# Last down pair of the second feed-forward by seven block products, and the attention projection's sums moved from GpSimd to VectorE with three low parts by transfers

## The chip, the cores and the metric

The kernel runs on one core of one Trainium2 chip. The metric is device time in microseconds (us) of one execution, lower is better. Before the change the median of three runs is 1553.24 us (1552.8 to 1553.64). TensorE (PE) multiplies matrices, VectorE (DVE), ScalarE (ACT) and GpSimd (POOL) work elementwise, and SyncE (SP), ACT and POOL issue DMA transfers from their instruction queues.

## The reference

One layer of a streaming encoder runs over 576 columns: 512 prompt frames and 64 frames of a running stream. Cut to what matters here:

```python
def swiglu_ffn(x, w_gu, w_down):
    gate, up = jnp.split(x @ w_gu, 2, axis=-1)
    return (jax.nn.silu(gate) * up) @ w_down
...
    y_att = o.reshape(b, t, ATT_WIDTH) @ p['w_att_proj']
    merged = jax.nn.sigmoid(g_ml) * y_ml + jax.nn.sigmoid(g_att) * y_att
...
    h = layer_norm(ALPHA * h + mix, p['ln2_g'], p['ln2_b'])
    h = layer_norm(ALPHA * h + 0.5 * swiglu_ffn(h, p['ffn2_w_gu'], p['ffn2_w_down']), p['ln3_g'], p['ln3_b'])
```

The model width is 1024 (8 tiles of 128), the hidden width of a feed-forward 2816 (22 tiles). The change touches two products: the attention projection `o @ w_att_proj`, and the down projection of the second feed-forward with the layer norm after it, which gives the output `y`.

## The kernel before, in words

Activations lie transposed, features on the 128 partitions and the 576 columns along the free dimension. A product in 32-bit floats is made from three faster matmuls: weights and activations are both split into a high part (a copy rounded to the fast type) and a low part (the rest), and hi·hi, hi·lo and lo·hi are summed in PSUM. A high part is one ACT copy. A low part is one DVE subtraction, or, with `add_lo` (line 196), a second ACT copy with scale -1 and then a transfer issued on POOL that adds the source to it.

**Seven products.** Where a weight block of 2 x 2 quarters multiplies an activation block of 2 x 2 quarters, the kernel forms seven quarter products in place of eight, from sums of weight quarters and sums of activation quarters. `seven` (line 1115) does it for two output tiles of a down projection over the hidden tiles 8 to 15, with column halves of 288 (`A` and `B`); `Units.run` does it for gate and up, for input columns, and, as `Projection`, for the attention projection. `Combos` holds the activation sums: `add` (line 787) makes, for block i, a sum tile u (parts t1 and t3) and a sum tile v (parts t2 and t4), each out of two operations on 288 columns.

**The order of the work.** PE's instructions stand in program order; a small planner (`Order`) keeps a model clock of PE and lets delayed callbacks (`later`, `od.bg`) run as PE's matmuls are emitted. The other engines are ordered by a scheduler with priorities (`hot`, `tc.high_priority`), and each then works through its own queue in that order: what waits at the head holds all that is behind it. Weights come in by `pump` (line 233): SP loads a raw tile `wr` (two buffers), ACT and DVE split it into `wh` and `wl` (four buffers, `NWB`). The planned list is written out in `plan_ffn` (line 382). Tiles of 576 columns called `s` come from a pool of 24 slots (line 99); a new tile must wait until the last reader of the slot's old tile is done.

**The attention projection.** While PE still runs the gates `("in", 64+j)`, the background generator `os_split` (line 1806) splits the attention output `OT` into `oh` and `os`, and makes the sums and their parts, the tiles `tx`, with `halves` (line 1823): in each block i first v (`halves(i, 1)`, tile `o`), then u (`halves(i, 0)`, tile `s`). The u sums of the blocks 1 to 3 are begun on POOL by `begin` (line 780), one block ahead, and every low part is a DVE subtraction. Then lines 1855 to 1858 load two gate tiles `s<-gd` on ACT's queue, and `un.run(tail)` starts PE on the projection: a11·b11, a12·b21, the next unit's a11·b11, then s2·t2 (reads all four v tiles), s1·t1 and s3·t3 (read all four u tiles).

**The end of the second feed-forward.** The output tiles 0 to 5 are done by `plain` and `seven`. The last two, 6 and 7, are done by plain `gemm`s in the order (6, columns 0:320), (7, 0:320), (6, 320:576), (7, 320:576), each over 22 hidden tiles, three matmuls each; the six weight chunks are loaded and split twice, once for each column range. `collect` (line 559) adds a finished product to the residual tile and to the sums of the norm. After the first column range, `stats` (line 648) runs while PE is in the second: small matmuls `aux<-onec`, a chain ACT `m`, DVE `var`, POOL `rs`, ACT `dg` and `c`, then `centre` (line 713) on DVE and POOL, a matmul `aux<-dg` (`spread`), and eight `apply` steps (DVE `s<-s,cols,aux`, ACT, and a transfer `out_y` each). The second column range ends with `turned` (line 682): sums, transposes, eight DVE steps and four transfers `out_yt`; nothing comes after it.

## Time and profile before

| | |
|---|---|
| profiled execution, device time | 1553.24 us |
| its span, first to last instruction | 1551.5 us |
| time around the span | 1.7 us |
| granted TensorE clock | 0.998 |
| PE / DVE / ACT / POOL busy in the span | 1530.7 / 1140.2 / 891.7 / 234.7 us |
| matmul instructions | 11579 |

The profiled execution is at the median of the three runs. A row of the timeline has the start, the duration, the engine, the line, the operation, the tile written and the tiles read with their shapes, and in brackets the engine's idle time ahead of it and who ended it; `x2` merges equal neighbours. Tile names in a profile have no numbers: `s<-o` is a u sum, `o<-s,o` a v sum, `tx<-...` a part of either.

### The profile page before, as it was taken

The page shows a single profiled execution, that of the slowest core. Times are in us where ns is not written, and L with a number is a line of the kernel's source. Part 1 is how long each engine was busy: PE and PEld are TensorE (multiplying, and loading weights), DVE is VectorE, ACT ScalarE, POOL GpSimd, SP SyncE. Part 2 cuts the span into 40 slices and gives each one's busy share as a digit, 9 for nine tenths or more (in the row PEclk, how much of TensorE's full clock was granted, in tenths as well). Part 3 has the DMA queues.
Part 4 walks back from the last instruction along what each step waited for, and adds up shares of the span by engine and source line. Part 5 has one row for each costly group of instructions (what it writes and reads, how often), then busy time and mean ns, then how long its engine had stood idle before and what let it go on. Part 6 is the DMA issues. An engine that isn't in the chain of part 4 may idle for free.

```text
span 1551.5 us, 29498 instructions
## 1 busy us (share of the span) xinstructions
PE 1530.7 (99%) x11579; PEld 1516.1 (98%) x11579; DVE 1140.2 (73%) x2103; ACT 891.7 (57%) x1700; POOL 234.7 (15%) x437
## 2 busy tenths in 40 slices
PE   9999999999999999999999999999999999999998
PEld 9999999999899999999999999999999999999997
DVE  7877778675988766777586766755776877788756
ACT  7544457442866557777754877753456454457333
POOL 1000000000310015555311222202121000001000
PEclk9999999999999999999999999999999999999999
DMA  9232323533754438687534765642755323226334
GB/s 262 108 109 83 105 86 93 142 108 89 204 150 155 137 130 223 153 204 188 120 137 137 189 145 138 163 144 82 210 141 128 109 82 109 82 72 145 119 113 150
DMA packets 80260, 211.15 MB, mean 136 GB/s; under 512 B 9081, under 2 KB 20985, under 8 KB 80121
## 3 DMA queue, kind: packets, MB, share of 16 engines
q1 hardware_dynamic: 65144, 169.15, 33.3%
q0 software_dynamic: 11808, 34.28, 12.7%
q10 hardware_dynamic: 3168, 5.83, 1.1%
q8 instruction: 91, 1.49, 0.4%
q14 instruction: 49, 0.39, 0.1%
HBM read 172.27 MB, written 21.63 MB: 125 GB/s over the span
## 4 chain that ended last, share of the span: by engine, by line
PE 87%; DVE 4%; ACT 4%; DMA 2%; POOL 1%; issue 1%; SPq 0%; ACTq 0%; DVEq 0%; POOLq 0%
PE mm L135 70%; PE aux L135 15%; PE aux L145 2%; DVE s L152 1%; ACT sc L149 1%; DVE wl L152 1%; DVE sc L1585 1%; DMA s<-in_xT 1%; ACT s L149 1%; DMA G<-in_rbias 1%; ACT wh L149 0%; POOL kh L159 0%; DMA wr<-in_w_gu 0%; ACT wh L872 0%; DVE s L155 0%
## 5 line engine op out<-in xcount | busy, mean ns | idle before, releaser
L135 PE MATMUL mm<-s,wh 128*128 128x288 f32 (+2 forms) x3667 | 752.2, 298 | 6.9 <-DVE s L152 3.1
L135 PEld LDWEIGHTS mm<-s,wh 128*128 128x128 f32 x3667 | 588.0, 189 | 11.4 <-DVE s L152 2.3
L135 PE MATMUL mm<-s,wl 128*128 128x288 f32 (+2 forms) x1806 | 533.1, 295 | 0.0
L135 PEld LDWEIGHTS mm<-s,wl 128*128 128x128 f32 x1806 | 340.0, 188 | 0.0
L149 ACT ACTIVATE wh<-wr 128x1024 fp32r<-128x1024 f32 (+2 forms) x143 | 134.0, 948 | 156.7 <-PE mm L135 91.3
L152 DVE TENSOR_TENSOR wl<-wr,wh 128x1024 fp32r<-128x1024 f32 (+2 forms) x93 | 107.5, 1164 | 49.0 <-ACT wh L149 48.6
L135 PE MATMUL mm<-tx,wh 128*128 128x288 f32 x677 | 140.3, 296 | 0.8 <-DVE tx L152 0.8
L135 PEld LDWEIGHTS mm<-tx,wh 128*128 128x128 f32 x677 | 109.2, 188 | 1.2 <-DVE tx L152 1.0
L152 DVE TENSOR_TENSOR wl<-wt,wh 128x1024 fp32r<-128x1024 f32 x51 | 62.5, 1225 | 55.8 <-ACT wh L872 55.8
L135 PE MATMUL mm<-tx,wl 128*128 128x288 f32 x350 | 103.2, 295 | 0.0
L872 ACT ACTIVATE wh<-wt 128x1024 fp32r<-128x1024 f32 x51 | 54.1, 1060 | 83.1 <-DVE wt L152 83.1
L152 DVE TENSOR_TENSOR wl<-wu,wh 128x1024 fp32r<-128x1024 f32 x63 | 77.1, 1223 | 31.3 <-ACT wh L872 31.3
L872 ACT ACTIVATE wh<-wu 128x1024 fp32r<-128x1024 f32 x63 | 66.7, 1058 | 41.2 <-PE mm L135 34.3
L135 PE MATMUL mm<-tx,ah 128*128 128x288 f32 x416 | 85.4, 297 | 0.4 <-ACT st L149 0.4
L198 POOL DMA_DIRECT2D s<-s x16 | 13.7, 854 | 469.4 <-DVE hb L152 426.7
L149 ACT ACTIVATE h<-h 128x288 f32<-128x288 f32 x78 | 34.0, 436 | 60.9 <-DVE h L152 60.9
L135 PEld LDWEIGHTS mm<-tx,ah 128*128 128x128 f32 x416 | 66.2, 188 | 1.2 <-ACT st L149 0.6
L135 PEld LDWEIGHTS mm<-tx,wl 128*128 128x128 f32 x350 | 65.7, 188 | 0.0
L152 DVE TENSOR_TENSOR ws<-wu 128x1024 f32<-128x1024 f32 (+1 forms) x55 | 64.7, 1176 | 0.0
L152 DVE TENSOR_TENSOR wl<-ws,wh 128x1024 fp32r<-128x1024 f32 x51 | 62.2, 1219 | 3.0 <-ACT wh L872 3.0
L135 PE MATMUL mm<-h,wh 128*128 128x288 f32 (+2 forms) x304 | 62.7, 296 | 0.1
L135 PE MATMUL mm<-tx,al 128*128 128x288 f32 x208 | 61.1, 294 | 0.0
(398 smaller groups left out, 3481.8 us busy)
## 6 DMA issues: line engine op xcount, KB each, us to landing
wu<-in_w_gu SPq DMA_DIRECT2D x78, 512.0 KB, 4.4
wr<-in_w_in SPq DMA_DIRECT2D x48, 512.0 KB, 4.2
wr<-in_w_dn SPq DMA_DIRECT2D x37, 512.0 KB, 3.8
wl<-in_w_in POOLq DMA_DIRECT2D x36, 512.0 KB, 6.3
wu<-in_w_in SPq DMA_DIRECT2D x24, 512.0 KB, 4.5
wr<-in_w_dn SPq DMA_DIRECT2D x19, 384.0 KB, 3.2
s<-s POOLq DMA_DIRECT2D x16, 288.0 KB, 4.4
wu<-in_w_ap SPq DMA_DIRECT2D x8, 512.0 KB, 4.7
```

What stands on the lines that cost most here:

```text
L135: PE.matmul(out, lhsT, rhs, start=start, stop=stop, **kw)
L145: PE.transpose(out, in_, idn)
L149: return ACT.activation(out, in_, func, **kw)
L152: return (eng or DVE).tensor_tensor(out, a, b, op=op)
L198: return POOL.dma_start(lo, src, accum_op=ALU.add)
L872: self.last = ACT.activation(hi, src, AF.Copy)
L1585: DVE.tensor_tensor_reduce(out=out, in0=ps, in1=g, op0=ALU.add, op1=ALU.min, scale=1.0, scalar=3e38, accum_out=acc)
```

## The change

In the attention projection `begin` is gone: the u and v sums of all four blocks are four DVE operations in `add`, and the slot for a block's u sum is taken when its own block is made, not one block ahead. The low parts of u for the blocks 0 to 2 are made by `add_lo`, that is by a second ACT copy and a transfer on POOL's queue; the low part of block 3's u and all of v's stay on DVE.

In the second feed-forward the tiles 6 and 7 are done by `seven` over the hidden tiles 8 to 15, and by one `gemm` over the other 14 hidden tiles (`Outer`), in the same order of four passes. Its four weight chunks are split once and held until their second pass. The norm's `spread` comes 3000 ns (was 4920 ns) of planner time after `stats`, and the eight `apply` steps are emitted 650 ns apart (were 860 ns).

```diff
@@ plan_ffn
-        for r in range(2):
-            for j in (6, 7):
-                for c in range(3):
-                    chunk(j, c)
+        seven(6)
+        for j in (6, 7):
+            chunk(j, 0)
+            chunk(j, 2)
@@ Norm.spread
-                later(860 * j, lambda j=j: self.apply(j, hf, rb))
+                later((860 if self.final is None else 650) * j, lambda j=j: self.apply(j, hf, rb))
@@ Combos
-        def begin(self, i):
-            r1, r2 = self.raw[4 + i], self.raw[i]
-            a, b = slice(0, HT_), slice(HT_, T)
-            u = self.sums[2 * i]
-            tt(u[:, a], r1[:, a], r1[:, b], ALU.subtract, POOL)
-            tt(u[:, b], r2[:, b], r1[:, b], ALU.subtract, POOL)
...
-            if not begun:
-                tt(u[:, a], r1[:, a], r1[:, b], ALU.subtract)
+            tt(u[:, a], r1[:, a], r1[:, b], ALU.subtract)
             stt(v[:, a], u[:, a], -1.0, r2[:, b], ALU.mult, ALU.subtract)
-            if not begun:
-                tt(u[:, b], r2[:, b], r1[:, b], ALU.subtract)
+            tt(u[:, b], r2[:, b], r1[:, b], ALU.subtract)
             return stt(v[:, b], v[:, a], -1.0, r2[:, a], ALU.mult, ALU.subtract)
@@ ffn, end of the second
-                    for hf in range(2):
-                        ln.residual(6, hf)
-                    for j, hl in [(j, (hf,)) for hf in (0, 1) for j in (6, 7)]:
-                        gemm([[((f"dn{n}", j, c), nk) for c, (_, nk) in enumerate(DC)]], hp_, [ln.cb(j)], (((0,), hl),))
+                    ln.spread_at = 3000
+                    Y, Z = seven(n, 6, inner, ln)
+                    for ps, cc in ((Y, A), (Z, B)):
+                        ln.take(6, cc, ps, ALU.add)
+                    for j in (7, 6):
+                        ln.whole(j)
+
+                    class Outer(Act):
+                        def get(self, k, hf):
+                            return hp_.get(k if k < KT else k + KT, hf)
+
+                    gemm([[((f"dn{n}", j, c), DC[c][1]) for c in (0, 2)] for j in (6, 7)], Outer(), [ln.cb(j) for j in (6, 7)],
+                         (((0,), (0,)), ((1,), (0,)), ((0,), (1,)), ((1,), (1,))))
@@ os_split
                     act(hi, t)
-                    tt(lo, t, f(hi), ALU.subtract)
+                    if n or i == 3:
+                        tt(lo, t, f(hi), ALU.subtract)
+                    else:
+                        add_lo(lo, hi, t)
...
                 for i in range(4):
-                    if i == 0:
-                        combos.sums[0] = slot(F32)
-                    if i < 3:
-                        combos.sums[2 * i + 2] = slot(F32)
-                        combos.begin(i + 1)
-                    combos.add(i, i > 0)
+                    combos.sums[2 * i] = slot(F32)
+                    combos.add(i)
                     halves(i, 1)
                     yield None
                     halves(i, 0)
```

How the queues of the engines change is shown at three places. First DVE's queue in the projection, where the blocks 2 and 3 are summed. Before (`s_9993` and `s_10033` are the u sums of blocks 2 and 3, made by POOL; `o_8983` and `o_9379` become v; `tx_10053` is the low part of block 3's v, which PE reads last in s2·t2):

```order
L155 SCALAR_TENSOR_TENSOR o_8983<-s_9993,o_7489 128x288 [waits Pool_49]
L152 TENSOR_TENSOR tx_10012<-s_9958,tx_10011 128x576 [waits Activation_49]
L155 SCALAR_TENSOR_TENSOR o_8983<-o_8983,o_7489 128x288 [waits DVE_49,Pool_49]
L155 SCALAR_TENSOR_TENSOR o_9379<-s_10033,o_7895 128x288 [waits Pool_49]
L155 SCALAR_TENSOR_TENSOR o_9379<-o_9379,o_7895 128x288 [waits DVE_49,Pool_49]
L152 TENSOR_TENSOR tx_10039<-o_8983,tx_10038 128x576 [waits Activation_49]
...
L152 TENSOR_TENSOR tx_10053<-o_9379,tx_10052 128x576 [waits Activation_49]
```

After (`s_10032` and `s_10050` are the u sums of blocks 2 and 3, and `tx_10056` is block 3's low part of v):

```order
L152 TENSOR_TENSOR s_10032<-o_8983 128x288 [waits DMASW2_49]
L152 TENSOR_TENSOR s_10032<-o_7489,o_8983 128x288
L155 SCALAR_TENSOR_TENSOR o_8983<-s_10032,o_7489 128x288 [waits DVE_49]
L155 SCALAR_TENSOR_TENSOR o_8983<-o_8983,o_7489 128x288 [waits DVE_49]
L152 TENSOR_TENSOR wl_10113<-wu_9851,wh_10112 128x1024 [waits DMASW1_49,DMASW5_49,PE_49,Activation_49]
L152 TENSOR_TENSOR tx_10038<-o_8983,tx_10037 128x576 [waits Activation_49]
L152 TENSOR_TENSOR o_10075<-mm_10090,o_10075 128x288 [waits PE_49]
L152 TENSOR_TENSOR s_10050<-o_9379 128x288 [waits DMASW3_49]
...
L155 SCALAR_TENSOR_TENSOR o_9379<-o_9379,o_7895 128x288 [waits DVE_49]
L152 TENSOR_TENSOR wu_9854<-wu_9854 128x512 [waits DVE_49]
L152 TENSOR_TENSOR wu_9854<-ws_10132,wu_9854 128x512 [waits DVE_49]
L152 TENSOR_TENSOR tx_10056<-o_9379,tx_10055 128x576 [waits Activation_49]
```

The two sums now stand on DVE, and the first operation of each waits on a transfer's semaphore: DMASW2 and DMASW3 are those on which PE waits for the low parts of the u sums of blocks 0 and 1, whose slots the new tiles take. The whole of DVE's queue stands behind these two waits.

Second, ACT's queue at the end of the same stage. Before, from the parts of block 3's v on:

```order
L149 ACTIVATE o_10072<-mm_10071 128x288 [waits PE_49]
L149 ACTIVATE tx_10052<-o_9379 128x576 [waits DVE_49]
L1858 DMA s_10064<-gd_4645 128x576 [waits DMAHW6_49,DVE_49]
L149 ACTIVATE tx_10056<-s_10033 128x576 [waits Pool_49]
L149 ACTIVATE o_10114<-aux_10113 128x288 [waits PE_49]
```

After (`tx_10042` is the third low part made by a transfer, on POOL's queue, with semaphore DMASW4; `tx_10059` is the high part of block 3's u):

```order
L149 ACTIVATE tx_10041<-s_10032 128x576
L149 ACTIVATE tx_10042<-tx_10041 128x576 [waits Activation_49]
L149 ACTIVATE o_10117<-aux_10116 128x288 [waits PE_49]
L149 ACTIVATE tx_10055<-o_9379 128x576 [waits DVE_49]
L1857 DMA s_10067<-gd_4645 128x576 [waits DMAHW6_49,DMASW4_49,DMASW2_49]
L149 ACTIVATE tx_10059<-s_10050 128x576
```

The load of the gate tile takes the slot of block 2's u sum, so it waits for the third transfer, and the copy of block 3's u stands behind it on ACT.

Third, DVE's queue in the last column range of the second feed-forward, from the last `centre` step on. Before:

```order
L152 TENSOR_TENSOR wl_18990<-wr_18905,wh_18989 128x1024 [waits DMAHW7_49,PE_49,Activation_49]
L152 TENSOR_TENSOR wl_19024<-wr_18963,wh_19023 128x768 [waits DMAHW2_49,PE_49,Activation_49]
L155 SCALAR_TENSOR_TENSOR s_17570<-s_17570,cols,aux_19005 128x320 [waits DVE_49,PE_49]
L152 TENSOR_TENSOR s_18117<-mm_18897,s_18117 128x256 [waits PE_49]
L155 SCALAR_TENSOR_TENSOR s_17564<-s_17564,cols,aux_19005 128x320 [waits DVE_49]
L152 TENSOR_TENSOR s_2670_17562<-s_2670_17562,s_18117 128x256 [waits DVE_49]
```

After:

```order
L152 TENSOR_TENSOR s_18120<-mm_18942,s_18120 128x256 [waits PE_49]
L152 TENSOR_TENSOR s_2670_17565<-s_2670_17565,s_18120 128x256 [waits DVE_49]
L155 SCALAR_TENSOR_TENSOR s_17573<-s_17573,cols,aux_19022 128x320 [waits PE_49]
L152 TENSOR_TENSOR s_2671_17566<-s_2671_17566,sq_19014 128x256 [waits Activation_49]
L155 SCALAR_TENSOR_TENSOR s_17567<-s_17567,cols,aux_19022 128x320
...
L155 SCALAR_TENSOR_TENSOR s_18122<-s_18122,cols,aux_19022 128x320 [waits Pool_49]
L152 TENSOR_TENSOR s_18122<-mm_19018,s_18122 128x256 [waits PE_49]
```

The two weight splits are gone; the collect of tile 6, and then all eight `apply` steps, still stand ahead of the collect of tile 7, the last row, as they did before.

More of the change, by code (lines that the diff above doesn't have):

```diff
@@ L778, in tile, with add @@
             return slot(F32R, self.pool, "tx", bufs=self.nx) if self.n <= self.nx else slot(F32R)
-        def begin(self, i):
-            r1, r2 = self.raw[4 + i], self.raw[i]
-            a, b = slice(0, HT_), slice(HT_, T)
-            u = self.sums[2 * i]
-            tt(u[:, a], r1[:, a], r1[:, b], ALU.subtract, POOL)
-            tt(u[:, b], r2[:, b], r1[:, b], ALU.subtract, POOL)
-        def add(self, i, begun=False):
+        def add(self, i):
             r1, r2 = self.raw[4 + i], self.raw[i]
```

## Prediction

> **What bounds the kernel now.** I read the page first, then the waits of PE, then the two stages that the diff touches.
>
> ```profile
> span 1551.5 us, 29498 instructions
> PE 1530.7 (99%) x11579; PEld 1516.1 (98%) x11579; DVE 1140.2 (73%) x2103; ACT 891.7 (57%) x1700; POOL 234.7 (15%) x437
> ```
>
> PE is busy 99% of the span: a change pays if it takes matmuls off PE, takes away one of PE's few waits, or shortens the time after PE's last matmul; a new wait of PE costs its full length. The waits of PE that lie in the two stages are these, by total, times and longest:
>
> ```profile
> PE mm L135 <- DVE tx L152: 0.8, 1, 0.8
> PE aux L135 <- DVE s L152: 0.4, 1, 0.4
> ```
>
> The first is in the projection. Its place, and PE's next reads, from the timeline of PE:
>
> ```profile
> 795.32 0.29 PE L135 MATMUL mm<-oh,wl 128*128 128x288 f32 x1
> ...
> 799.80 0.29 PE L135 MATMUL mm<-tx,wh 128*128 128x288 f32 x1
> 800.89 0.40 PE L135 MATMUL mm<-tx,wh 128*128 128x288 f32 x1 [0.79 <-DVE tx L152]
> 802.04 0.43 PE L135 MATMUL mm<-tx,ah 128*128 128x288 f32 x2
> 802.44 0.42 PE L135 MATMUL mm<-tx,ah 128*128 128x288 f32 x2
> ```
>
> At 795.61 the first product is done and ACT may copy it. At 799.80 PE takes block 3's high part of v, at 800.89 its low part, late by 0.79; from 802.44 it takes block 3's u, whose low part it needs one matmul later, at 802.57 (three matmuls take 802.44 - 802.04 = 0.40, so one is 0.133). So DVE's queue sets PE here. Its rows:
>
> ```profile
> 784.26 0.45 DVE L152 TENSOR_TENSOR s<-o 128x288 f32<-128x288 f32 x1
> 784.63 0.45 DVE L152 TENSOR_TENSOR s<-o,o 128x288 f32<-128x288 f32 x1
> ...
> 791.02 1.37 DVE L152 TENSOR_TENSOR tx<-o,tx 128x576 fp32r<-128x576 f32 x1
> ...
> 797.31 1.22 DVE L152 TENSOR_TENSOR wl<-wu,wh 128x1024 fp32r<-128x1024 f32 x1
> 798.45 0.75 DVE L152 TENSOR_TENSOR tx<-s,tx 128x576 fp32r<-128x576 f32 x1
> 799.11 0.68 DVE L152 TENSOR_TENSOR ws<-wu 128x512 f32<-128x512 f32 x1
> ...
> 800.08 0.75 DVE L152 TENSOR_TENSOR tx<-o,tx 128x576 fp32r<-128x576 f32 x1
> ```
>
> Start to start, a sum of 288 columns takes 0.37, a weight split 1.14, a part of 576 columns 0.66, a sum of 512 some 0.61. The row at 791.02 took 1.37 instead of 0.75: POOL was summing beside it.
>
> ```profile
> 790.58 1.19 POOL L152 TENSOR_TENSOR s<-o 128x288 f32<-128x288 f32 x1 [17.29 <-DVE tx L152]
> 794.12 0.96 POOL L152 TENSOR_TENSOR s<-o 128x288 f32<-128x288 f32 x1 [1.06 <-DVE tx L152]
> ```
>
> POOL had waited for DVE's parts to give slots back. The second stage is the end, in three windows: columns 0:320 of tiles 6 and 7, columns 320:576, and what follows the last matmul (the number behind the window is its length, then PE busy):
>
> ```profile
> 1502.60:1522.20 19.60, 19.60 (x136) 19.60 (x135) 10.42 (x15) 6.96 (x9) 0.00 (x0) 1.00 0.48 142
> 1522.20:1540.90 18.70, 18.31 (x153) 17.91 (x151) 13.29 (x24) 8.85 (x18) 3.15 (x3) 1.00 0.45 153
> 1540.90:1551.50 10.60, 3.46 (x31) 3.22 (x31) 5.96 (x10) 0.65 (x3) 0.70 (x1) 0.78 0.31 113
> ```
>
> PE never waits in the first, 0.39 in the second. The last 10.6 us are a chain of small steps that the change leaves alone.
>
> **The projection, step by step.** All times are on before's clock. Removed are six POOL sums; added are six DVE sums (0.37 each, 2.2 us), three ACT copies (0.68 each) and three transfers in place of three DVE parts (0.66 each, 2.0 us). So DVE's work is even, and it no longer runs at half pace beside POOL. What counts is order: the u sums of blocks 2 and 3 take slots that the first and second transfer must have read. What a transfer takes, from the view of POOL's transfers into tiles `s` (whole run; two with nothing beside them, at 1409.7 and 1412.6; two issued behind weight loads, with SP's and POOL's rows there):
>
> ```profile
> L198 POOL DMA_DIRECT2D s<-s x16: 841/858/859, 250.4 to 1424.1; - x16
> DMA to landing us min/median/max: 3.4/4.8/6.9
> ...
> DMA to landing us min/median/max: 3.4/3.4/3.4
> ...
> DMA to landing us min/median/max: 5.3/5.4/5.5
> ...
> 1416.56 1.20 SPq L252 DMA_DIRECT2D wr<-in_w_dn  x2
> ...
> 1418.03 0.84 POOL L198 DMA_DIRECT2D s<-s  x1 [4.58 <-ACT s L149]
> ```
>
> So 3.4 alone, 5.4 behind two weight loads, 6.9 at worst, from the issue. How long POOL takes from ACT's copy to an issue, then ACT's rows, and SP's next weight load:
>
> ```profile
> 756.31 0.88 POOL L198 DMA_DIRECT2D wl<-in_w_in  x1 [0.25 <-ACT wl L149]
> ...
> 788.79 0.68 ACT L149 ACTIVATE tx<-s 128x576 fp32r<-128x576 f32 x1
> ...
> 796.88 0.40 ACT L149 ACTIVATE o<-mm 128x288 f32<-128x288 f32 x1
> ...
> 799.23 0.33 ACTq L1858 DMA_DIRECT2D s<-gd  x1
> ...
> 798.56 0.80 SPq L864 DMA_DIRECT2D wu<-in_w_ap  x2
> ```
>
> First transfer: ACT's copy of block 0's u starts at about 789.0 (788.79, and 0.2 because block 0's v ends one weight split later); the second copy ends at 790.4, the issue is 0.25 later, and with no load on SP's queue until its row at 798.56 it lands 3.4 later, at 794.1. Meanwhile DVE sums block 1 from 790.5 to 792.2 (four sums, a dependent one at its full 0.45), waits for ACT's copy (0.7), makes the part and is free at 793.7: it waits 0.4. Second transfer: block 1's u is copied from 792.8 to 794.2; issue near 794.5, landing 797.9.
>
> Block 2's sums then run from 794.1 to 795.8. ACT copies its v until 796.6 (it first copies PE's result, the row at 796.88, ready from 795.61 on) and its u twice until 797.9: the third issue is at 798.2. DVE splits weights until 796.9, and this frees the buffer for SP's two loads, at 796.95 instead of 798.56, 1.25 us ahead of the third transfer. That is the case of the row at 1418.03, 1.47 behind its first load, so I take 5.5: landing 803.7.
>
> Block 3's sums start at 798.0, after block 2's part, a result and the second landing. Four sums and one of 512 between them end at 800.2; two more sums of 512, one waiting for the other, stand ahead of the part, which starts at 801.5 and ends at 802.2. PE gets it at 802.3 instead of 800.89: **+1.4**, whatever the third transfer does.
>
> The third transfer decides what comes next: ACT's load `s<-gd` (0.33) waits for it, and behind it stands the copy of block 3's u (0.68), then DVE's part (0.75): 803.7 + 0.4 + 0.7 + 0.75 + hand-overs = 805.6, against the 802.57 at which PE took it: **+3.1 in all**, which contains the 1.4. Bounds: with a landing in 3.4 us (801.6) the 1.4 stands alone; with 6.9 (805.1) it is +4.5; if the first two also need the median 4.8, another 1.3. Below +1.4 I find no way, since the second landing cannot come before 797.9 by these rows. What follows cannot absorb it, since PE is busy there without a gap:
>
> ```profile
> 820.00:870.00 50.00, 50.00 (x383) 49.95 (x383) 32.95 (x55) 30.43 (x61) 11.28 (x36) 1.00 0.51 155
> ```
>
> The Trainium skill, page "DMA: Bandwidth & Descriptors", section "Anatomy of one DMA — SWDGE (gpsimd) path", fits such a transfer as 2.0 us plus the bytes at 436 GB/s, so an estimate of 2.7 us for 288 KB, at any load; by it this stage would cost +1.1 and the sum below would give 1554.1 us. The fastest of this trace, 3.4 us, speaks against it, and I give it 3 in 100, inside rival two.
>
> **The end, step by step.** On PE, the hidden tiles 8 to 15 cost 96 matmuls before (48 of 320 columns, 48 of 256) and 84 of 288 after. A matmul of 320 takes 19.60 / 132 = 0.148; one of 288 takes 0.133; one of 256 about 0.119 (the second window less 2.6 us of norm matmuls and wait, over 132, gives 0.122). So the part before the switch to columns 320:576 lasts 84 x 0.133 + 84 x 0.148 = 23.6 instead of 19.6, **+4.0**, and PE's part after it is 48 x 0.119 = 5.7 shorter. With the wait of 0.39 gone PE would be done 4.0 - 5.7 - 0.4 = -2.1, earlier by 2.1 us. The splits for it (eight in place of twelve, plus four DVE sums) lie beside PE: DVE is busy 10.42 of 19.60 in the first window, and each chunk is wanted no sooner than before.
>
> But the second range now gives DVE less time than its chain needs. Its rows, with PE's wait:
>
> ```profile
> 1525.08 0.83 PE L135 MATMUL aux<-onec,s 128*128 128x1 f32 x6 [0.39 <-DVE s L152]
> ...
> 1528.59 3.87 DVE L152 TENSOR_TENSOR s<-s,c 128x320 f32<-128x320 f32 x6 [2.28 <-ACT c L149]
> ...
> 1535.64 0.41 DVE L152 TENSOR_TENSOR s<-s,s 128x256 f32<-128x256 f32 x1
> 1535.97 0.41 DVE L152 TENSOR_TENSOR s<-s,sq 128x256 f32<-128x256 f32 x1
> 1536.31 2.83 DVE L155 SCALAR_TENSOR_TENSOR s<-s,cols,aux 128x320 f32<-128x320 f32 x6
> 1540.91 0.42 DVE L152 TENSOR_TENSOR s<-mm,s 128x256 f32<-128x256 f32 x1 [1.78 <-PE mm L135]
> ```
>
> From PE's row at 1525.08 to the first `s<-s,c` it is 3.5 us (ACT, DVE and POOL in turn, unchanged); six of those take 3.8 until the next may start; tile 6's collect is three rows, 1.1 with one dependence; eight `apply` at 0.46 (2.83 for six, less the overlap) take 3.7. The last collect, which stands behind all of them in the queue, can start 12.1 after PE's row. Before, it started 15.8 after it and had waited 1.78 for PE; after, PE would be ready 10.1 after it, so **DVE is late by 2.0**. PE's row itself comes 2.45 after the range starts (2.88 before, less the wait). So the last collect starts at 4.0 + 2.45 + 12.1 = 18.55 against 1540.91 - 1522.20 = 18.7: **-0.2**. The smaller spacing of `apply` in the planner does not help, since the queue, not the planner, holds the order. Bounds: -2.1 if DVE keeps up after all, +0.5 if a weight chunk or an ACT copy is late by a row.
>
> **The sum.** 1553.24 + 3.1 - 0.2 = 1556.1 us. The profiled execution (span 1551.5 and 1.74 around it) is itself the median, so nothing is to be converted. A measurement of this kernel can tell about 0.2%, 3.1 us, from no change: faster is below 1550.1, slower above 1556.35, and the forecast lies just inside.
>
> **Rivals.** *One, slower:* the transfers meet more load than I took. The loads that start at 796.95 may also catch the second one, and the third may need 6.9. For it speaks that the slowest of this trace, 6.9, is of the same kind; against it, that the second is nearly landed by then. With 6.9, +4.5 - 0.2 gives 1557.5; with a late second as well, 1558.8. It decides from a third landing after 803.9 on, 5.7 us.
>
> *Two, quiet transfers:* the third finds the loads already done and lands by 802, so that only the 1.4 is left: 1553.24 + 1.4 - 0.2 = 1554.4. The idle DMA queues between 781 and 798 speak for it, the earlier weight load against it.
>
> *Three, PE sets the end:* DVE's rows after the norm run faster than I add up, and the 2.1 of PE arrive: 1553.24 + 3.1 - 2.1 = 1554.2. For it: two of the six `s<-s,c` rows are slow only because POOL runs beside them. Against it: POOL still does.
>
> *Four, faster:* both stages give what they promise. PE's wait of 0.8 goes and the end shortens by 2.1: 1550.3. This needs the slots not to be in the way; the queue of after shows the waits on the transfers, which speaks against it. That the end does not do what it says, saving nothing, is already my forecast.
>
> **How the numbers follow.** Forecast (third landing at 803.1 to 803.9, end near 0) 45 in 100; one 25; two 15; three 8; four 7. Slower by over 0.2% are rival one and the upper part of the forecast, 17 of its 45: 0.42. Faster by over 0.2% is what four holds below 1550.1: 0.05. The rest, 0.53, is within. The range from 1552.4 to 1558.8 takes in rival one with a late second transfer above, and two and three together below (1553.24 + 1.4 - 2.1 = 1552.5); it leaves out rival four and what lies beyond one, some 12 in 100.
>
> **What would show it.** In the projection, DVE's `s<-o` rows should wait for `DMA tx<-s`, ACT's `s<-gd` should stand near 803.7 with idle time ahead of it, and PE should wait 1 to 2 us twice, for `tx` near 800 and again near 804; PE's window 820 to 860 should then be the old one, 3 us later. At the end the last `s<-mm,s 128x256` should have no idle time on DVE, and PE should idle about 2 us ahead of `aux<-onec,s`. I am wrong if PE's wait in the projection is under 1 us in all, or if the time from 1480 to the end shrinks by more than 1 us.

## The result, and the profile after

The changed kernel takes 1559.63 us (median of 5, 1559.08 to 1561.44) against 1553.64 us for the kernel before in the same rounds (1552.8 to 1554.07): ratio 1.0041, 95% interval 1.003 to 1.0052. It is slower by 6.0 us; the forecast was 2.9, with the range up to 1558.8. The profiled execution took 1559.08 us with a span of 1556.7, 5.2 more than before. The spans of the five executions are 1556.7, 1557.9, 1556.6, 1558.3 and 1558.7, so they differ among themselves by 2 us; those of the kernel before differ as much (1550.7 to 1553.8 in the rounds of e1 below), so a difference of 1 us between two single profiles proves little. The time around the span grew too: it was 1.7 us before and is 1.7 to 2.9 here, with a median of 2.5.

The span and the busy times on the page, then PE's new waits among its waits (engine, line, releaser: total, times, longest):

```profile
span 1556.7 us, 29461 instructions
...
PE 1531.7 (98%) x11567; PEld 1516.8 (97%) x11567; DVE 1140.3 (73%) x2111; ACT 890.8 (57%) x1699; POOL 231.8 (15%) x434
```
```profile
PE mm L135 <- ACT tx L149: 3.0, 1, 3.0
PE aux L135 <- DVE s L152: 1.6, 1, 1.6
...
PE mm L135 <- DVE tx L152: 0.9, 1, 0.9
```

PE's busy time is 1 us more than before, the span 5.2: most of it is waiting. The first and the third wait lie in the projection, the second at the end. PE in the projection:

```profile
795.65 0.29 PE L135 MATMUL mm<-oh,wl 128*128 128x288 f32 x1
...
803.25 0.40 PE L135 MATMUL mm<-tx,wh 128*128 128x288 f32 x1 [2.95 <-ACT tx L149]
804.53 0.61 PE L135 MATMUL mm<-tx,wh 128*128 128x288 f32 x1 [0.88 <-DVE tx L152]
...
807.34 0.68 PE L135 MATMUL mm<-tx,ah 128*128 128x288 f32 x2
```

The row at 795.65 was at 795.32 before: 0.33 had been lost by then, before PE reaches the projection. Block 3's u, the last row, was at 802.44: 4.90 later, so the projection costs 4.57 (the forecast said 3.1). PE waits 2.95 + 0.88 = 3.8 us instead of 0.8; the rest is in how fast it then runs. Three windows (the number ahead of the DMA share is the granted clock):

```profile
801.00:804.50 3.50, 0.40 (x1) 0.19 (x1) 3.46 (x8) 0.68 (x1) 0.00 (x0) 1.00 0.73 195
804.50:807.96 3.46, 3.43 (x14) 3.43 (x15) 1.54 (x3) 1.93 (x3) 0.00 (x0) 0.51 0.33 88
807.96:811.00 3.04, 3.04 (x25) 3.04 (x24) 2.07 (x3) 1.04 (x2) 0.00 (x0) 1.00 0.38 97
```

In the second window PE is busy throughout and does 14 matmuls in 3.46 us; at 0.133 each that is 1.9 us of work. The granted clock is half. Who made PE wait: the three transfers on POOL, SP's two weight loads, then DVE and ACT.

```profile
791.08 0.85 POOL L198 DMA_DIRECT2D tx<-s  x1 [19.07 <-ACT tx L149]
794.94 0.85 POOL L198 DMA_DIRECT2D tx<-s  x1 [3.00 <-ACT tx L149]
798.55 0.84 POOL L198 DMA_DIRECT2D tx<-s  x1 [2.77 <-DVE o L152]
```
```profile
797.41 1.32 SPq L855 DMA_DIRECT2D wu<-in_w_ap  x2
```
```profile
800.31 0.46 DVE L152 TENSOR_TENSOR s<-o 128x288 f32<-128x288 f32 x1 [1.89 <-DMA tx<-s]
...
803.72 0.75 DVE L152 TENSOR_TENSOR tx<-o,tx 128x576 fp32r<-128x576 f32 x1
...
806.51 0.76 DVE L152 TENSOR_TENSOR tx<-s,tx 128x576 fp32r<-128x576 f32 x1 [1.44 <-ACT tx L149]
```
```profile
802.51 0.68 ACT L149 ACTIVATE tx<-o 128x576 fp32r<-128x576 f32 x1 [2.95 <-DVE o L155]
805.41 0.33 ACTq L1857 DMA_DIRECT2D s<-gd  x1
805.79 0.68 ACT L149 ACTIVATE tx<-s 128x576 fp32r<-128x576 f32 x1 [2.60 <-DMA tx<-s]
```

The second transfer, issued at 794.94, holds DVE until 800.31; the third, issued at 798.55, holds ACT until 805.41. The chain that ended last names the second one with its length:

```profile
794.94 5.35 DMA tx<-s
804.53 5.25 PE mm L135 x26
```

At the end, DVE's last collect has no idle time and PE waits for it, as forecast:

```profile
1545.69 0.42 DVE L152 TENSOR_TENSOR s<-mm,s 128x256 f32<-128x256 f32 x1
```
```profile
1546.16 0.61 PE L135 MATMUL aux<-onec,s 128*128 128x1 f32 x4 [1.64 <-DVE s L152]
```

It was at 1540.91: 4.78 later where the projection left 4.90, so up to the last collect the end gains 0.1 (forecast 0.2) in this execution. What follows the collect takes longer than before. DVE's last rows before the change, then after:

```profile
1545.73 2.73 DVE L155 SCALAR_TENSOR_TENSOR s<-s,rs,s 128x512 f32<-128x512 f32 x4
```
```profile
1550.52 2.73 DVE L155 SCALAR_TENSOR_TENSOR s<-s,rs,s 128x512 f32<-128x512 f32 x4
```

They end 7.55 after the start of the collect in both. But the span ends 3.08 after them before and 3.44 after the change. The same two numbers, 3.07 to 3.08 and 3.43 to 3.45, stand in all nine profiles of this case with the old end and in all eleven with the new one. The traces show where it is spent: when the last output has landed, 2.1 after its issue, SP has two semaphore waits left with the old end and eight with the new one, 0.06 each. So the new end gives 0.37 back behind its last step. The parts add up to the span's 5.2: 0.33 + 4.57 - 0.12 + 0.37 = 5.15.

### The profile page after: what moved, and what is told of

The parts are those of the page before. It is cut to its first block, busy times and chain, and to the rows that moved or that the text cites. A ratio compares the mean times of both kernels' runs of the same rounds, so it can differ in the third digit from the quotient of the medians.

```text
span 1556.7 us, 29461 instructions
## 1 busy us (share of the span) xinstructions
PE 1531.7 (98%) x11567; PEld 1516.8 (97%) x11567; DVE 1140.3 (73%) x2111; ACT 890.8 (57%) x1699; POOL 231.8 (15%) x434
## 4 chain that ended last, share of the span: by engine, by line
PE 78%; issue 8%; DVE 6%; ACT 5%; DMA 1%; POOL 1%; SPq 0%; DVEq 0%; ACTq 0%; POOLq 0%
PE mm L135 64%; PE aux L135 12%; PE aux L145 2%; DVE s L152 1%; DVE s L155 1%; DVE wl L152 1%; ACT sc L149 1%; ACT s L149 1%; ACT wh L149 1%; POOL kh L159 0%; DVE sc L1585 0%; DMA wr<-in_w_gu 0%; ACT wh L863 0%; DMA wu<-in_w_ap 0%; DMA w<-in_w_gu 0%
## 5 line engine op out<-in xcount | busy, mean ns | idle before, releaser
L149 ACT ACTIVATE wh<-wr 128x1024 fp32r<-128x1024 f32 (+2 forms) x138 | 129.0, 947 | 148.6 <-PE mm L135 80.7
L152 DVE TENSOR_TENSOR wl<-wr,wh 128x1024 fp32r<-128x1024 f32 (+2 forms) x88 | 101.8, 1167 | 41.3 <-ACT wh L149 41.0
L863 ACT ACTIVATE ah<-wu 128x512 fp32r<-128x512 f32 x51 | 32.2, 631 | 47.4 <-PE mm L135 42.8
```

Source lines behind the costliest of these rows:

```text
L149: return ACT.activation(out, in_, func, **kw)
L152: return (eng or DVE).tensor_tensor(out, a, b, op=op)
L863: self.last = ACT.activation(hi, src, AF.Copy)
```

## The experiments

Times are medians beside the kernel before on the same chip; with each stands its ratio and 95% interval. 0.001 of the time is 1.55 us, and a difference with a sign is taken from the ratio, unless the text says otherwise. "Before's end" and "before's projection" mean that part of the change undone.

**e1 and e2: one part each.**

```diff
e1: plan_ffn, Norm.spread, ffn as changed; Combos and os_split as before
e2: Combos and os_split as changed; plan_ffn, Norm.spread, ffn as before
```

> The end of the second feed-forward as changed, the projection as before. Theory A (the whole loss is in the projection; at the end DVE's queue holds the last collect, so that PE's 2.1 us come to nothing): the last collect 0.2 us earlier against the start of this stage, 1553.4 us, within 0.5 of the kernel before. Theory B (the end loses too, since the 0.4 us between the last collect and the span's end in the profile after is real and belongs to it): 1554.0 to 1555.0. Rival C (the end pays its 2 us and the projection costs 8): 1551.3.

> The projection as changed, the end as before. Theory A: all of the loss, +4.6 us of span by the profile after and up to 6 where TensorE's granted clock stays low for longer: 1557.8 to 1559.8 us. Theory B: about 1 us less than the changed kernel, 1558.5. Rival C: 1561.5.

e2: 1558.17 against 1554.1, ratio 1.0028 (1.0016 to 1.0039), +4.4 us. e1: 1555.43, ratio 1.0009 (1.0 to 1.0018), +1.4 us. Together 5.8, the whole of the loss within the intervals: theory B, the end loses too, and by more than the 0.4 that theory B names. By the medians of the executions, e1 is 0.8 us longer than the kernel before in its span (1553.1 against 1552.3) and 0.8 longer around it (2.50 against 1.74). What makes the time around the span longer is open. Of the 0.8 in the span, 0.37 are SP's last waits. More is in e1's trace, PE and the window after its last collect (which starts at 1540.93, where it was before):

```profile
1538.82 0.95 PE L135 MATMUL aux<-onec,s 128*128 128x1 f32 x8
1541.40 1.02 PE L135 MATMUL aux<-onec,s 128*128 128x1 f32 x4 [1.63 <-DVE s L152]
```
```profile
1540.90:1553.70 12.80, 5.38 (x24) 4.98 (x24) 6.25 (x11) 1.25 (x5) 0.70 (x1) 0.51 0.39 141
```

The same small steps take 12.8 us instead of 10.6, at a clock of 0.51: four small matmuls last 1.02 and not 0.61, and DVE's last step ends 9.29 after the start of the collect and not 7.55. So the low clock costs 1.7 in this execution. In the profiled execution of the changed kernel they took 11.0:

```profile
1545.70:1556.70 11.00, 2.98 (x24) 2.70 (x24) 5.95 (x11) 1.21 (x5) 0.70 (x1) 0.79 0.45 164
```

Here the clock fell only after PE's work was done. How much of the differences between executions is due to this is not shown. In the changed kernel the spans of 1557.9 to 1558.7 have mean clocks of 0.994 to 0.996, those near 1556.6 have 0.997 and 0.998. But in e1 the six executions with a mean clock of 0.997 or less have a median span of 1553.3, the five others one of 1553.1.

**e3: no transfers.**

```diff
-                    if n or i == 3:
-                        tt(lo, t, f(hi), ALU.subtract)
-                    else:
-                        add_lo(lo, hi, t)
+                    tt(lo, t, f(hi), ALU.subtract)
```

> The projection with its sums on DVE as changed, but all low parts on DVE again, no transfers; the end as before. Theory A1 (DVE's queue is full either way, and the transfers only replace work by waits): by adding up the queue's rows from 784.7 on, block 3's v part is ready near 803.5 instead of 800.9, PE waits 3.4 us in one piece and may lose the clock as well: +2.6 to +4.1, 1555.8 to 1557.4 us. Rival A2 (the transfers' landings are the entire cause): no loss, 1553.4.

1558.06, ratio 1.0024 (1.0014 to 1.0034), +3.7 us: theory A1. Block 3's v part starts at 803.18, PE waits 2.1 and 0.9 us, and its clock is low for 6.85 us:

```profile
803.00:809.85 6.85, 5.96 (x25) 5.86 (x25) 3.44 (x5) 2.33 (x4) 0.00 (x0) 0.50 0.16 43
```

So moving the sums to DVE costs about as much without the transfers (+3.7) as with them (+4.4): the transfers do take work off DVE, and give it back as waits.

**e4 and e12: buffers of their own.** In e4 the gate loads go to SP's queue as well, in e12 they stay on ACT's.

```diff
-                    combos.sums[2 * i] = slot(F32)
+                    combos.sums[2 * i] = slot(F32) if i < 2 else osp.tile([P, T], F32, tag="ux", name=nm("ux"), bufs=2)
e4 only:
-        ACT.dma_start(sg[j], GD[j])
+        SP.dma_start(sg[j], GD[j])
```

> The projection as changed with its three transfers, but the u sums of the blocks 2 and 3 in two buffers of their own, so that DVE waits for no landing, and the two gate loads on SP's queue, so that ACT waits for none; the end as before. Theory A1 (landings hold back DVE and ACT through the slots): DVE gains 2.3 us, PE's wait of 2.95 us shrinks to about 1 and its clock stays up; what is left is PE's own read of the third transfer's part, landed near 804.5: +1 to +2.4, 1554.3 to 1555.8 us. Rival A3 (the slots don't matter, DVE's work alone is too long): +4 or more, 1557.5.

> The kernel of e4 (own buffers for the u sums of the blocks 2 and 3) with the gate loads back on ACT's queue, so that SP's two weight loads again start beside the third transfer, and ACT waits for the second landing. Theory A1: the third transfer takes 6 to 7 us again, from about 797.9 to 804.5, and PE reads its part 2 us late; DVE's wait is gone: 1555.0 to 1556.0 us. Rival (only the slots held DVE and ACT back, the landing itself is hidden): as e4, 1553.6.

e4: 1553.63, ratio 0.9997 (0.9988 to 1.0006): the loss is gone, more than expected. e12: 1560.28 against 1554.0, ratio 1.0037 (1.0024 to 1.0049), +5.7 us, worse than expected. In neither does DVE wait for a landing (with buffers of their own, its queue even has the first sums of the blocks 2 and 3 much earlier). The two differ in the third transfer. In e4, SP's gate loads wait for the landings and hold the weight loads behind them back, past the third issue at 797.87; PE waits half a microsecond:

```profile
793.88 6.31 SPq L1848 DMA_DIRECT2D s<-gd  x2
800.35 0.81 SPq L855 DMA_DIRECT2D wu<-in_w_ap  x2
```
```profile
801.31 0.40 PE L135 MATMUL mm<-tx,ah 128*128 128x288 f32 x1 [0.49 <-DMA tx<-ux]
```

In e12 the third transfer is issued at 800.06 (some 0.5 us later against PE's work than in e4, since ACT's gate loads wait for landings ahead of its copies), the weight loads start beside it, and PE waits for it directly (and gets the low clock on top):

```profile
800.48 0.81 SPq L855 DMA_DIRECT2D wu<-in_w_ap  x2
```
```profile
806.58 0.61 PE L135 MATMUL mm<-tx,ah 128*128 128x288 f32 x1 [3.35 <-DMA tx<-ux]
```

The third transfer took 3.4 us in e4 and 6.5 in e12.

**e8 and e11: idle matmuls into PE's wait in the projection**, to keep the clock up. 

```diff
e8, inside product() of the projection's first s2 t2, ahead of block 3:
+                for _ in range(30 if fill is not None and i == 3 else 0):
+                    PE.matmul(fill[:, 384:512], ones_r, ones_r, start=True, stop=True, skip_group_check=True)
e11: range(12 ...), start=False, stop=False
```

In e8 and in e5 below, the idle matmuls start a new accumulation in the bank of the sums beside them, which therefore lack earlier terms (`y` is off by a relative 1.8 in e5 and 0.37 in e8); in e9, e11 and e14 they only add to unused columns.

> The kernel of e2 (projection as changed, end as before) with 30 idle matmuls of 128 columns, some 1.8 us, ahead of block 3's first product, where PE waits 2 to 3 us. Theory G (the third transfer's landing, through ACT's gate load and block 3's u, is what PE must reach in the end; the low clock fills a wait that would be there anyway): the clock stays up, but a new wait of 1 to 1.5 us stands ahead of block 3's u, and the time is that of e2, 1557.5 to 1558.5 us. Rival H (the low clock costs its 1.4 us on top): 1556.6.

> The kernel of e2 with 12 idle matmuls (1.3 us) in PE's wait of 2 to 3 us ahead of block 3's first product; e8 had 30, which took 3.3 us and more than filled the wait. Theory G (what PE must reach in the end is block 3's u part, released by the third landing through ACT's gate load): the clock stays up and a wait of 0.5 to 1.5 us stands ahead of block 3's u; the time is e2's, within 0.5: 1557.7 to 1558.5 us. Rival H (the low clock costs 1.4 us on top): 1556.7.

e8 misses: 1560.66 against 1553.8, ratio 1.0048 (1.0034 to 1.0061). An idle matmul took 0.11 us and not 0.06, so that 30 outlasted the wait. e11 fits: 1558.0 against 1554.0, ratio 1.0024 (1.0016 to 1.0033), where e2 had 1.0028, with the clock at 1.00 throughout the projection in its profile. PE's row at block 3's u in e11:

```profile
805.98 0.40 PE L135 MATMUL mm<-tx,ah 128*128 128x288 f32 x1 [0.40 <-DVE tx L152]
```

PE works at full pace from 803.40 and runs into the third landing instead. This is theory G: in this execution the low clock would have been hidden behind the third transfer. Rival H is not excluded. The idle matmuls may have kept the clock up in some executions only: three of e11's eleven have a mean clock of 0.999, as 23 of 26 of the kernel before have, and their median span is 1555.3 against 1556.4 of the eight others.

**e13 and e14: the third landing taken away, the second left.** e13 is e2 with the gate loads on SP; e14 adds e11's 12 idle matmuls.

> The kernel of e2 (projection as changed, slots and all) with only the two gate loads moved to SP's queue, where they wait for the third landing and so hold back the two weight loads behind them: the third transfer runs alone and lands 3.4 us after its issue, near 801.9, and ACT is not held. DVE still waits for the second landing. Theory J (two chains of nearly equal length: the second landing, late by one of its sixteen parts, makes PE wait 2 to 3 us, and the low clock then stretches PE to where the third landing would have let it go): almost all of the loss stays, 1557.0 to 1558.0 us. Rival K (the third landing is the cause, the second is not): 1554.5 to 1555.5.

> The kernel of e13 with e11's 12 idle matmuls in PE's wait, which keep the clock up. Theory J: the low clock's 1.4 us, hidden behind the third landing in e11, is now saved: 1555.6 to 1556.6 us. Rival K: as e13, or worse by the idle matmuls that no longer fit.

e13: 1557.25 against 1554.1, ratio 1.0023 (1.0014 to 1.0032), +3.6 us. Its premise was half wrong: the weight loads stand ahead of the gate loads in SP's queue, so the third transfer still took 5.3 us; but neither ACT nor PE waits for it any more. PE waits only for what the second landing holds back (2.90 us, then 0.88), and its clock falls. So the second landing with the clock costs nearly as much as all three: theory J, two chains of nearly equal length. e14 misses theory J's figure: 1557.98, ratio 1.0023 (1.0014 to 1.0033), as e13. The clock fell in its profile in spite of the idle matmuls, so it does not test theory J further.

**e5 and e9: idle matmuls into PE's wait at the end.**

```diff
e5, on e1, in turned(), between the sums that are ready and those of the last collect:
+                if s is dh:
+                    for _ in range(24):
+                        PE.matmul(st[:, P:2 * P], ones_r, ones_r, start=True, stop=True, skip_group_check=True)
e9: range(10), start=False, stop=False
```

> The kernel of e1 (end as changed, projection as before) with 24 idle matmuls of 128 columns, some 1.4 us of work whose result nobody reads, put on PE's queue into its wait of 1.63 us for the last collect. Theory D (in e1 PE's wait at the end lets the granted clock fall to about half, and the chain after the last collect takes 12.8 us instead of 10.6): the clock stays up, 10.6 again, 1553.4 us, 1.5 to 2 less than e1. Rival E (the clock is an accident of e1's profiled run, or its cause lies earlier): no difference to e1, 1555.4.

> The kernel of e1 with 10 idle matmuls in PE's wait at the end in place of e5's 24, which took 0.11 us each and not the 0.06 assumed, and so outlasted the wait by 1 us. 10 take 1.1 us of the 1.63. Theory D (the low clock after PE's wait at the end is what the end part costs): the clock stays up behind the collect in most runs, 10.7 us from the last collect to the end of the span, 1553.6 us in median, 1 to 1.5 less than e1. Rival E: as e1, 1555.1 to 1555.4.

e5: 1555.09 against 1553.8, ratio 1.001 (1.0001 to 1.0019). The clock stayed up in its profile, but the 24 ended 1 us after the collect, so the gain was spent. e9: 1555.0 against 1554.0, ratio 1.0004 (0.9995 to 1.0013), between theory D and its rival and nearer to the rival by the medians; in its profile the clock fell all the same. Neither bears out theory D. Their spans are 1.5 and 1.3 longer than those of the kernel before (1553.4 against 1551.9, 1553.3 against 1552.05), where e1's was 0.8; what they lack is e1's longer time around the span (1.72 and 1.74). These two do not show the size of the clock's part.

**e6, e10: the last collect ahead in DVE's queue.**

```diff
e6, on e1:
-                    ln.spread_at = 3000
-                later((860 if self.final is None else 650) * j, lambda j=j: self.apply(j, hf, rb))
+                later(860 * j, lambda j=j: self.apply(j, hf, rb))
e10, on e6, in moments() of tile 6 (early() issues the small sums of the tiles 0 to 6):
+            elif hf and self.final is not None and j == KT - 2:
+                later(3000, self.early)
```

> The kernel of e1 with the planner's times as before the change (spread 4920 ns after the sums, apply steps 860 ns apart), so that the last collect stands behind five apply steps in DVE's queue, and three come after it. Theory D: the collect starts 1.4 to 1.7 us earlier, PE waits under 0.5 us and keeps its clock, and the three steps fit into DVE's idle 1.5 us after the collect: 1551.7 to 1552.0 us. Rival F (what DVE saves ahead of the collect it pays behind it): 1553.4.

> The kernel of e6 with the first half of the small sums of the end (those of the tiles 0 to 6, one column wide) issued 18 wide matmuls before PE's last product ends, not after it: the wide matmuls end 0.4 us later, PE's wait for the collect goes, and the stretch of small matmuls in which the clock may fall is 0.9 us shorter. Theory D: the collect as in e6, and the clock falls less often: 1551.9 to 1552.6 us, up to 1.5 less than the kernel before. Rival (the clock falls anyway, since after the last wide matmul all that PE has is small): as e6, level with the kernel before.

e6: 1553.64 against 1553.8, ratio 0.9998 (0.9989 to 1.0007): the loss of e1 is gone, and the gain of theory D does not show; the time is rival F's. In its profile the collect does start earlier, 79.73 us after the matmul `aux<-dr,ones_r` that opens this stage, against 80.92 in e1 and 81.14 before. The clock still falls behind it (0.62 over the last 11 us), but costs nothing there: DVE's last step ends 7.55 after the start of the collect, as before. With the 0.37 of SP's waits its stage is 1.0 shorter than before in this profile, which is within the interval. e10: 1553.26 against 1554.0, ratio 0.9995 (0.9986 to 1.0004); DVE in e10, with five steps ahead of the collect and three behind it:

```profile
1537.51 2.38 DVE L155 SCALAR_TENSOR_TENSOR s<-s,cols,aux 128x320 f32<-128x320 f32 x5
1540.53 0.42 DVE L152 TENSOR_TENSOR s<-mm,s 128x256 f32<-128x256 f32 x1 [0.64 <-PE mm L135]
1540.87 1.46 DVE L155 SCALAR_TENSOR_TENSOR s<-s,cols,aux 128x320 f32<-128x320 f32 x3
```

The collect waits for PE again, not PE for the collect.

**e7, e15 to e18: versions to which the runs point.** e7 is e4's projection with e6's end, e16 (repeated as e18) e4's projection with e10's end, e15 is e10 with PE's order changed in the projection, e17 is e16 with two transfers in place of three.

```diff
e15:
+                if ahead is not None and isinstance(self, Projection):
+                    self.second(ahead)
                 self.product(new["X"], j, "s2", "t2", False, False)
e17:
-                    if n or i == 3:
+                    if n or i >= 2:
```

> The projection of e4 (own buffers for two u sums, gate loads on SP) and the end of e6. If the two are independent: 1553.4 less 1.0 (e4's span against the kernel before) less 1.5: 1550.9 us, faster than the kernel before by 0.16%. If the saved time at the end is lost to the clock: 1552.4 or more.

> The kernel of e10 (projection as before the change) with the second unit's product a12 b21, 12 matmuls or 1.6 us that need none of the sums, moved ahead of s2 t2 on PE, whose wait of 0.8 us for block 3's part it can fill. If the 0.8 us and PE's slow restart of 0.2 us after it go: 1 us less than e10, 1552.3 us. If the units behind it now wait for their weight splits instead: as e10, 1553.3.

> The projection of e4 (own buffers, gate loads on SP) and the end of e10. If the two gains add (0.5 and 0.7 us): 1552.8 us, the kernel before less 1.2.

> e16 once more, to measure it against the kernel before in further rounds. As in e16: 1.1 us less than the kernel before, within 0.7.

> The kernel of e16 with block 2's low part of u back on DVE, so that only two transfers are left and PE waits for none. DVE has 0.66 us more, beside 2.2 us in which e4's DVE waits between 792 and 797. If that hides it: PE's wait of 0.5 to 1.2 us for the third landing goes, 0.5 less than e16, 1552.5 us. If DVE's queue is late with block 3's v by the 0.66 instead: as e16.

e7: 1553.35 against 1553.8, ratio 1.0001 (0.9992 to 1.001), a miss: in its profile the clock fell 2.7 us after the start of the last wide matmul, and the end took 11.9 us from the collect on. e15: 1554.54 against 1554.1, ratio 1.0004 (0.9995 to 1.0013), a miss: the 12 matmuls only moved PE's waits to later places (1.35 and 0.50 us). e16: 1552.97 against 1554.1, ratio 0.9995 (0.9986 to 1.0004), and e18 1553.24 against 1554.58, the same ratio and interval. e17: 1552.31 against 1554.58, ratio 0.999 (0.9981 to 0.9999): the one version whose interval lies below the kernel before, by 0.1% (2.3 us by the medians, 1.6 by the ratio). As the best of eighteen, with an interval that ends next to 1, this is weak evidence. In the projection its PE does not wait at all:

```profile
797.00:810.00 13.00, 13.00 (x99) 12.79 (x98) 11.54 (x17) 7.22 (x12) 0.00 (x0) 1.00 0.47 135
```

## Why the prediction was wrong, point by point

**The places were right.** DVE's u sums wait for landings (1.89 us at block 3), ACT's `s<-gd` stands behind the third landing, PE waits for `tx` twice, from 800.3 and near 804 (2.95 and 0.88 us, where 1 to 2 were named), the last collect has no idle time on DVE, and PE idles 1.64 us ahead of its sums.

**The step that failed first: "landing 797.9" for the second transfer and "so I take 5.5" for the third.** They took 5.35 and 6.8 us, landing at 800.3 and 805.35. Their issues, at 794.94 and 798.55, came as forecast within 0.1, but for the 0.33 that had been lost before. The trace before held slower transfers of this size than the 6.9 taken as the worst: five into tiles `tx`, from 418 to 434, took 5.8 to 7.7, while the forecast read only those into tiles `s`. The times are those of rival one with its late second transfer, but its reason, the weight loads, fits the third only, which SP's loads preceded by 1.1 us. The second was priced at 3.4 since nothing ran beside it; and fifteen of the sixteen completion marks that the trace has for it did come by 3.42, only the last at 5.35. In e4 it took 5.35 as well, and SP's weight loads started there at 800.35, after it had landed at 799.78. So the forecast of 1558.8 for rival one comes close to the time partly by luck. DVE waits for all sixteen. So DVE waits 1.89 us where the step had it go on at 798.0, and block 3's v reached PE at 804.53 and not 802.3. With 6.8 the third landing leads to 805.35 + 0.4 + 0.7 + 0.75 = 807.2, the 807.34 at which PE took block 3's u. The chain of steps holds, its two transfer times were too short: the term "+3.1" measured 4.57. e4, e12 and e13 show that both count: with the second alone in the way (e13) +3.6, with PE waiting for the third alone (e12) +5.7, with neither (e4) nothing.

**"+3.1" priced waits only.** The waits of 2.95 and 0.88 us also halved the granted clock for 3.41 us, here some 1.5 us of PE's time. In the changed kernel this is hidden behind the third landing as far as the profile of e11 shows; e11's executions leave room for a part of it. Where the second landing or DVE alone sets PE (e13, e3) it is part of the loss.

**"-0.2" at the end was right for the collect (80.92 after the opening of the stage, in e1 and in the changed kernel, against 81.14) and wrong for the time.** By e1 the part costs 1.4 us (interval 0 to 2.8). Three terms were put at nothing. "The last 10.6 us are a chain of small steps that the change leaves alone": SP's six further waits alone make it 11.0. PE's 2 us of idle time ahead of the last collect were counted as free: in e1's profile the clock fell in that wait, at 1541.18, which made the 11.0 into 12.8; how often and how much in other executions could not be measured separately (e5, e9). And "nothing is to be converted" left out the time around the span, which is 1.74 in the prediction and has a median of 2.5 in the changed kernel and in e1; why is open.

**"The smaller spacing of `apply` in the planner does not help, since the queue, not the planner, holds the order" was wrong.** With the planner's old times (e6, which undoes the spacing and the earlier `spread` together) three of the eight steps go behind the collect, it starts 1.2 us earlier, and e1's loss is gone. The planner's times are what made DVE late. (In the sum of this step, 2.88 less 0.39 is 2.49 and not 2.45, which changes nothing.)

**"DVE's work is even" held.** DVE is busy for 1140.3 us after and 1140.2 before, and e4, with the same work on DVE, loses nothing. Without the transfers, DVE has the 2.0 us of the three parts more, and the stage loses 3.7 (e3). The loss of the change is one of order and landings, not of work.

**Open** are the clock's own share at the end, the longer time around the span, and what makes the second landing late (below).

## What to carry to other kernels

A transfer that takes work off a busy engine must be followed to every reader of its slot and every queue that waits for its last part, and priced at its slow end if loads can start beside it; here buffers of their own for two sums, the gate loads on another queue, and one transfer less took all of PE's waits in the projection away. Where the last steps of a kernel are a chain, look which of the steps that nobody waits for stand ahead of it in the queue. A wait of TensorE is not only its own length: look at the granted clock in the windows behind it. And look behind the last step of the last engine, and at the time around the span: a change can lose there what it gains ahead of it.

## What the runs showed of the hardware

**The granted clock falls after waits shorter than 3.4 us.** In the profiles of e2 and e3, PE's waits of 2.0 and 0.9 us (2.1 and 0.9) with one matmul between them brought it to half; the low stretch lasted 3.41 us in the changed kernel (804.55 to 807.96) and twice that in e3. The Trainium skill, page "TensorE: Matmul & The Clock Gate", section "Part 1: The HAM clock gate (the "warmup" mystery)", gives an activity window of about 3.4 us that runs freely, and a fall after at least one idle window. The length of the low stretches agrees; the waits that were enough here are shorter than such a window. At the end of the kernel, where PE has only matmuls of one column or of 128, the fall came 2.5 us after the start of the last wide matmul in e1, 2.7 in e7, 3.3 in e9, 3.7 in e6, 8.6 in the changed kernel: it varies from run to run. In e1's profile it cost 1.7 us, in that of e6 nothing. In e7 the clock came back after 3.41 us:

```profile
1539.92:1542.33 2.41, 1.97 (x18) 1.83 (x18) 2.41 (x6) 2.23 (x6) 0.00 (x0) 1.00 0.76 266
1542.33:1545.74 3.41, 3.39 (x16) 2.99 (x15) 2.55 (x5) 1.13 (x4) 0.69 (x1) 0.50 0.56 196
1545.74:1549.16 3.42, 0.00 (x0) 0.00 (x0) 3.40 (x5) 0.00 (x0) 0.00 (x0) 1.00 0.33 125
```

**Where the clock can change.** The traces show when it does: in all twenty profiles every stretch between two changes, up to the last, is a whole number of 3.413 us (in the changed kernel 234, 1 and 218 of them; 2 in e3). This grid begins 4.0 to 10.6 us after the span's start, differently from profile to profile, so the same wait lies differently in it. Outside the end of the kernel, a clock that was up fell after the six steps of the grid in which PE was idle for 2.0 us or more (one each in e2, e3, e12, e13, e14 and the changed kernel), and stayed up after all in which PE was idle for 1.74 or less. e13 has both, one behind the other (PE busy is the number behind the length):

```profile
798.86:802.27 3.41, 1.67 (x13) 1.43 (x11) 1.78 (x5) 0.41 (x1) 0.76 (x1) 1.00 1.01 334
802.27:805.68 3.41, 1.38 (x8) 1.16 (x9) 3.38 (x7) 1.66 (x4) 0.00 (x0) 1.00 0.39 66
805.68:809.09 3.41, 3.41 (x16) 3.41 (x15) 2.16 (x3) 1.58 (x3) 0.00 (x0) 0.50 0.47 153
```

At the end it also fell after steps with 0.4 us of idle time (e6, e7), where PE had mostly matmuls of one column or of 128.

**The late sixteenth of the second transfer.** In all twelve profiles with transfers at this place, the last part of the second one lands 0.5 to 2.2 us after the fifteenth, and in each a fetch of instructions by DMA, of 0.9 to 1.9 us, falls into it. Into the first transfer no fetch falls, and its last part comes 0.02 to 0.04 after the fifteenth. In the changed kernel, between 796 and 799 (queue: packets, MB, share of 16 engines):

```profile
q8 instruction: 1, 0.02, 3.9%
```

One packet that takes 0.039 x 16 x 3.0 = 1.9 us on one engine, and the last part is 5.35 - 3.42 = 1.9 us late. In e13 and e14 the part is 2.1 and 2.2 us late with a fetch of only 0.9. That the fetch delays it is argued from this, not tried.

**What weight loads cost a transfer beside them.** The third transfer, of 288 KB, took 5.3 to 6.8 us where SP's two loads of 512 KB were issued ahead of it or at most 0.4 behind it (the changed kernel, e2, e8, e11 to e14), and 3.4 to 4.3 where they were issued 1.4 to 2.5 behind it (e4 with 3.40, e7, e16, e18).
